# Seven half-width products in place of eight for the gate/up matrix product of a two-layer decoder trunk, and the output product in four chunks

## The chip, the cores and the metric

The kernel runs on one core of a Trainium2 chip. The metric is the time of one execution in device microseconds, the median of several runs; the profile shows one execution in detail. The core has a matrix engine (TensorE, "PE"; its weight loads have a row of their own, "PEld"), VectorE ("DVE"), ScalarE ("ACT"), GpSimd ("POOL"), and SyncE ("SP"), which issues the transfers. Each engine works off its own queue in order; they wait for each other on semaphores.

## The reference

512 tokens of width 1024 go through two layers. A layer is an attention part (one input projection, four heads of differential attention, eight heads of stick-breaking attention, gates, output projections, residual) and then the part that matters here:

```
h2 = rms_norm(x, g_ffn)                                   # 512 x 1024
gate, up = jnp.split(h2 @ w_ffn_in, 2, axis=-1)           # 1024 x 5632 weights
x = x + (jax.nn.silu(gate) * up) @ w_ffn_out              # 2816 x 1024 weights
```

After the second layer comes a last `rms_norm`. All is float32.

## The kernel before

Tokens lie along the free axis: `xs[m]` is a 128x512 tile of `x` (128 channels, 512 tokens), and there are eight of them. Float32 accuracy comes from three matmuls per weight tile: weights and activations are split into a high part (a cast on ACT) and a low part (a subtraction on DVE), and `mm_tiles` (L199 to L206) issues high x high, low x high and high x low into one PSUM bank. `Norm.feed` (L167) makes the split tiles `h` of the scaled `x`; the row factor `r` of the norm comes only from `Norm.finish` (L189) and is multiplied in behind the product.

Weights stream from HBM in pieces of 128x1024 (`w_pieces`, L96): a transfer issued by SP into `wr` (two buffers), the cast to `wh` on ACT (L111), the low part `wl` on DVE (L113; four buffers each). `w_get` (L120) keeps two pieces ahead of the matmuls. `stream` fixes the order of the pieces.

The FFN of a layer (L611 to L642): for each of the 22 hidden tiles `j`, 24 matmuls of 512 columns for gate (`fg`) and 24 for up (`fu`); DVE multiplies both by `r` out of PSUM (L623, L625), ACT takes silu (L624), POOL the product (L626), ACT and DVE split it (L629, L630). Then each of the eight output tiles `fo` sums 22 hidden tiles in one bank (66 matmuls), DVE adds it to `xs[m]` (L639), and the next norm is fed. In the last layer the eighth output tile is done in two halves of 256 tokens (L643 to L665), so that the final norm and the output transfers of the first half run beside the second.

The order in which the instructions stand on each engine's queue is not the order of the code: a scheduler places them when the program is built, by costs of its own, and inserts the waits. Names that recur below: `wh`/`wl` high and low part of a weight piece; `fg`, `fu`, `fo` the PSUM banks of gate, up and output; `yf` the row factor `r`.

## Time and profile before

| | |
|---|---|
| median of 3 runs | 1525.14 us (1522.21 to 1525.25) |
| the profiled execution | 1526.8 us, span of the trace 1525.0 us |
| PE busy | 1488.5 us (98%), 6884 matmuls |
| DVE, ACT, POOL busy | 853.7, 614.4, 347.4 us (56, 40, 23%) |
| granted TensorE clock, mean | 0.988 |

A row of the profile gives engine, line, operation, the tile written and those read, how many, busy time and mean length. Matmuls overlap: a row's length includes the way through the array, so the pace is read from the starts of neighbours. An instruction that waits for a resource inside the engine (not for a semaphore) shows as a longer row.

### The profile page before, as it was taken

The page shows a single profiled execution, that of the slowest core. Times are in us where ns is not written, and L with a number is a line of the kernel's source. Part 1 is how long each engine was busy: PE and PEld are TensorE (multiplying, and loading weights), DVE is VectorE, ACT ScalarE, POOL GpSimd, SP SyncE. Part 2 cuts the span into 40 slices and gives each one's busy share as a digit, 9 for nine tenths or more (in the row PEclk, how much of TensorE's full clock was granted, in tenths as well). Part 3 has the DMA queues.
Part 4 walks back from the last instruction along what each step waited for, and adds up shares of the span by engine and source line. Part 5 has one row for each costly group of instructions (what it writes and reads, how often), then busy time and mean ns, then how long its engine had stood idle before and what let it go on. Part 6 is the DMA issues. An engine that isn't in the chain of part 4 may idle for free.

```text
span 1525.0 us, 17531 instructions
## 1 busy us (share of the span) xinstructions
PE 1488.5 (98%) x6884; PEld 1238.6 (81%) x6884; DVE 853.7 (56%) x1006; ACT 614.4 (40%) x970; POOL 347.4 (23%) x224
## 2 busy tenths in 40 slices
...
DMA packets 43619, 139.59 MB, mean 92 GB/s; under 512 B 5648, under 2 KB 8080, under 8 KB 43536
## 3 DMA queue, kind: packets, MB, share of 16 engines
...
## 4 chain that ended last, share of the span: by engine, by line
PE 90%; DVE 5%; issue 1%; ACT 1%; DMA 1%; POOL 0%; SPq 0%; DVEq 0%; POOLq 0%; ACTq 0%
PE fu L206 5%; PE fg L205 5%; PE fg L206 5%; PE fu L205 5%; PE fg L204 5%; PE fu L204 5%; PE fo L204 5%; PE fo L205 5%; PE fo L206 5%; PE pg L204 4%; PE pg L205 4%; PE pg L206 4%; PE pd L204 3%; PE pd L205 3%; PE pd L206 3%; PE wo L204 2%
## 5 line engine op out<-in xcount | busy, mean ns | idle before, releaser
L111 ACT CAST wh<-wr 128x1024 fp32r<-128x1024 f32 (+3 forms) x251 | 258.0, 1029 | 629.7 <-PE fu L206 157.5
L113 DVE TENSOR_TENSOR wl<-wr,wh 128x1024 fp32r<-128x1024 f32 (+2 forms) x229 | 329.8, 1440 | 216.7 <-ACT wh L111 216.1
L626 POOL TENSOR_TENSOR u<-u,g 128x512 f32<-128x512 f32 x44 | 56.8, 1292 | 441.5 <-DVE u L625 394.3
L205 PE MATMUL fo<-ah,wl 128*128 128x512 f32 (+1 forms) x374 | 141.0, 377 | 0.0
L204 PE MATMUL fo<-ah,wh 128*128 128x512 f32 (+1 forms) x374 | 141.0, 377 | 0.0
L206 PE MATMUL fo<-al,wh 128*128 128x512 f32 (+1 forms) x374 | 140.8, 377 | 0.0
L204 PE MATMUL fg<-hhf,wh 128*128 128x512 f32 x352 | 137.8, 391 | 0.0
L206 PE MATMUL fu<-hlf,wh 128*128 128x512 f32 x352 | 137.0, 389 | 0.0
L205 PE MATMUL fg<-hhf,wl 128*128 128x512 f32 x352 | 137.0, 389 | 0.0
L206 PE MATMUL fg<-hlf,wh 128*128 128x512 f32 x352 | 137.0, 389 | 0.0
L204 PE MATMUL fu<-hhf,wh 128*128 128x512 f32 x352 | 137.0, 389 | 0.0
L205 PE MATMUL fu<-hhf,wl 128*128 128x512 f32 x352 | 137.0, 389 | 0.0
L625 DVE TENSOR_TENSOR u<-fu,yf 128x512 f32<-128x512 f32 x44 | 30.4, 691 | 129.2 <-PE fu L206 129.2
L204 PE MATMUL pg<-hha,wh 128*128 128x512 f32 x256 | 100.5, 392 | 0.0
L205 PE MATMUL pg<-hha,wl 128*128 128x512 f32 x256 | 100.3, 392 | 0.0
L206 PE MATMUL pg<-hla,wh 128*128 128x512 f32 x256 | 100.2, 391 | 0.0
L206 PEld LDWEIGHTS fo<-al,wh 128*128 128x128 f32 x374 | 70.4, 188 | 13.0
L205 PEld LDWEIGHTS fo<-ah,wl 128*128 128x128 f32 x374 | 70.4, 188 | 12.9
L204 PEld LDWEIGHTS fo<-ah,wh 128*128 128x128 f32 x374 | 70.4, 188 | 12.9
L113 POOL TENSOR_TENSOR wl<-wr,wh 128x1024 fp32r<-128x1024 f32 (+3 forms) x22 | 51.9, 2360 | 124.9 <-ACT wh L111 120.4
L204 PE MATMUL pd<-hha,wh 128*128 128x512 f32 x192 | 78.2, 407 | 0.5 <-ACT knd3s L341 0.5
L205 PE MATMUL pd<-hha,wl 128*128 128x512 f32 x192 | 77.7, 405 | 0.0
...
## 6 DMA issues: line engine op xcount, KB each, us to landing
wr<-in_w_fi_dram SPq DMA_DIRECT2D x88, 512.0 KB, 3.6
wr<-in_w_in_dram SPq DMA_DIRECT2D x78, 512.0 KB, 3.7
wr<-in_w_fo_dram SPq DMA_DIRECT2D x32, 512.0 KB, 3.5
wr<-in_w_o_dram SPq DMA_DIRECT2D x16, 512.0 KB, 3.6
wr<-in_w_out_dram SPq DMA_DIRECT2D x16, 512.0 KB, 3.6
...
cs<-in_tab_dram SPq DMA_DIRECT2D x2, 512.0 KB, 5.4
```

What stands on the lines that cost most here:

```text
L111: nc.scalar.copy(out=hi[:, c], in_=raw[:, c])
L113: eng.tensor_tensor(out=lo[:, c], in0=raw[:, c], in1=f32(hi[:, c]), op=ALU.subtract)
L204: nc.tensor.matmul(dst, hi[:, c], rh, start=first and k == 0, stop=False)
L205: nc.tensor.matmul(dst, lo[:, c], rh, start=False, stop=False)
L206: nc.tensor.matmul(dst, hi[:, c], rl, start=False, stop=last and k == n - 1)
L625: nc.vector.tensor_tensor(out=u, in0=bu, in1=r, op=ALU.mult)
L626: nc.gpsimd.tensor_tensor(out=u, in0=u, in1=g, op=ALU.mult)
```

## The change

Only the FFN changes. The hidden tiles 0 and 1 stay as they were ("classic"). The other 20 are computed by the Strassen-Winograd scheme of seven products: the 1024 inputs are divided into even and odd tiles of 128 (four each), the outputs into gate and up, the 512 tokens into two halves. A product (`prod`) is four input tiles x three matmuls of 256 columns, 12 matmuls; seven of them stand in place of 48 matmuls of 512 columns.

For this, four sums of the activations are made once a layer (`sf`, `sh`, `sl`), and for each `j` four sums of the weights (`w_sums`): POOL makes `tf[0]`, `ru[0]`, `tf[1]`, `tf[2]` from the raw pieces `rg` and `ru`, and the split parts are `wh`/`wl` (of `rg`, later of `ru`), `tah`/`tal` (of `tf[0]` and `tf[1]`) and `tbh`/`tbl` (of `tf[2]`). `tf` and `tb` have one buffer. The products of a tile run in the order b11, t1, t2, b21, t3, then, behind the b11 of the next tile, t4 and b22. b11, t2, t3 and t4 go into one bank (`fa`); ACT copies it out after b11, t2 and t3 (`a`, `b`, `c`, 128x256 each), and the next product adds onto the bank. t1 and b22 go into `fc`, b21 into `fb`. DVE and POOL put gate and up together from these. `up` is no longer multiplied by `r`; instead the output product is (`add_x`).

The output product is done in four chunks of 6, 6, 5 and 5 hidden tiles, each behind the first tile of the next chunk. Each chunk's eight tiles are multiplied by `r` on DVE and added into `xs[m]`, on POOL for the first three chunks. Weight pieces of the output product are 768 or 640 columns, 32 a layer in place of 24. In the last layer the last chunk's tiles 4 to 7 are done in two halves of tokens.

```
+CHUNKS = ((0, 6), (6, 12), (12, 17), (17, 22))
+CLASSIC = 2
+EVEN_ODD = (0, 2, 4, 6, 1, 3, 5, 7)
+H = S // 2
...
-    layer_order += [("fi", j) for j in range(2 * NH)]
-    layer_order += [("fo", m, c) for m in range(8) for c in range(3)]
+    FFN = []
+    for c, (j0, j1) in enumerate(CHUNKS):
+        FFN.append(("j", j0))
+        if c:
+            FFN.append(("c", c - 1))
+        FFN += [("j", j) for j in range(j0 + 1, j1)]
+    FFN.append(("c", len(CHUNKS) - 1))
+    for kind, i in FFN:
+        if kind == "c":
+            layer_order += [("fo", m, i) for m in range(8)]
+        elif i < CLASSIC:
+            layer_order += [("fi", 2 * i), ("fi", 2 * i + 1)]
+        else:
+            layer_order.append(("fs", i))
...
+    def w_sums():
+        n = state["next"]
+        state["next"] = n + 1
+        l, _, j = stream[n]
+        fp = state["fp"]
+        pool, tag = (wp, "wr") if j % 2 else (fp, "wx")
+        rg = pool.tile([P, 2, 512], F32, name=f"rg{n}", tag=tag, bufs=2)
+        ru = pool.tile([P, 2, 512], F32, name=f"ru{n}", tag=tag, bufs=2)
+        for t, i in ((rg, 2 * j), (ru, 2 * j + 1)):
+            nc.sync.dma_start(out=t.rearrange("p a k -> p (a k)"), in_=w_fi[l, i])
+        tf = fp.tile([P, 3, 512], F32, name=f"tf{n}", tag="tf", bufs=1)
+        tt = lambda eng, o, a, b: eng.tensor_tensor(out=o, in0=a, in1=b, op=ALU.subtract)
+        def parts(src, pool, tag, bufs, shape):
+            hi = pool.tile(shape, F32R, name=f"{tag}h{n}", tag=tag if pool is wp else tag + "h", bufs=bufs)
+            lo = pool.tile(shape, F32R, name=f"{tag}l{n}", tag="wl" if pool is wp else tag + "l", bufs=bufs)
+            nc.scalar.copy(out=hi, in_=src)
+            nc.vector.tensor_tensor(out=lo, in0=src, in1=f32(hi), op=ALU.subtract)
+            return hi, lo
+        g = parts(rg, wp, "wh", W_BUFS, [P, 2, 512])
+        tt(nc.gpsimd, tf[:, 0], ru[:, 0], rg[:, 0])
+        tt(nc.gpsimd, ru[:, 0], ru[:, 1], ru[:, 0])
+        tt(nc.gpsimd, tf[:, 1], ru[:, 1], tf[:, 0])
+        tt(nc.gpsimd, tf[:, 2], rg[:, 1], tf[:, 1])
+        t = parts(tf[:, 0:2], fp, "ta", 2, [P, 2, 512])
+        u = parts(ru, wp, "wh", W_BUFS, [P, 2, 512])
+        v = parts(tf[:, 2], fp, "tb", 1, [P, 512])
+        at = lambda pr, i: (pr[0][:, i], pr[1][:, i])
+        ready.append((stream[n], dict(b11=at(g, 0), b21=at(g, 1), t1=at(t, 0), t2=at(t, 1), t3=at(u, 0), b22=at(u, 1),
+                                      t4=v), None))
     def w_prefetch():
+        if stream[state["next"]][1] == "fs":
+            return w_sums()
         for _ in w_pieces(1024):
             pass
     def w_get(*key):
-        while len(ready) <= W_AHEAD and state["next"] < len(stream):
+        while state["next"] < len(stream):
+            ahead = sum(2 if r[0][1] == "fs" else 1 for r in ready[1:])
+            if ready and ahead >= W_AHEAD:
+                break
             w_prefetch()
...
+            hq = [h[k] for k in EVEN_ODD]
...
+            for i in range(4):
+                he, ho = F("g", f"he{i}", 2), F("u", f"ho{i}", 2)
+                for t, k in ((he, 2 * i), (ho, 2 * i + 1)):
+                    nc.scalar.activation(out=t, in_=xs[k], func=AF.Copy, scale=pt[:, C_NF + 8 * l + k:C_NF + 8 * l + k + 1])
+                sf = F("wx", f"sf{i}", 2, (P, 4, H))
+                nc.vector.tensor_tensor(out=sf[:, 0], in0=he[:, H:], in1=ho[:, H:], op=ALU.add)
+                nc.gpsimd.tensor_tensor(out=sf[:, 2], in0=he[:, :H], in1=he[:, H:], op=ALU.subtract)
+                nc.vector.tensor_tensor(out=sf[:, 1], in0=sf[:, 0], in1=he[:, :H], op=ALU.subtract)
+                nc.vector.tensor_tensor(out=sf[:, 3], in0=ho[:, :H], in1=sf[:, 1], op=ALU.subtract)
+                sh, sl = F(f"sh{i}", f"sh{i}", 1, (P, 4, H), F32R), F(f"sl{i}", f"sl{i}", 1, (P, 4, H), F32R)
+                nc.scalar.copy(out=sh, in_=sf)
+                nc.vector.tensor_tensor(out=sl, in0=sf, in1=f32(sh), op=ALU.subtract)
+                for q in range(4):
+                    A[f"s{q + 1}"].append((sh[:, q], sl[:, q]))
...
+            def hidden(j, g, u):
                 silu = nc.scalar.activation(out=g, in_=g, func=AF.Silu)
-                nc.vector.tensor_tensor(out=u, in0=bu, in1=r, op=ALU.mult)
-                nc.gpsimd.tensor_tensor(out=u, in0=u, in1=g, op=ALU.mult)
-                hi = fp.tile([P, S], F32R, name=f"ah{j}_{l}", tag="a", bufs=2 * NH)
-                lo = fp.tile([P, S], F32R, name=f"al{j}_{l}", tag="a", bufs=2 * NH)
-                nc.scalar.copy(out=hi, in_=u)
-                nc.vector.tensor_tensor(out=lo, in0=u, in1=f32(hi), op=ALU.subtract)
-                act.append((hi, lo))
+                p = F("p", f"p{j}", 2)
+                (nc.vector if u.space == bass.MemoryType.PSUM else nc.gpsimd).tensor_tensor(
+                    out=p, in0=u, in1=g, op=ALU.mult)
+                hi, lo = F("a", f"ah{j}", 14, dt=F32R), F("a", f"al{j}", 14, dt=F32R)
+                nc.scalar.copy(out=hi, in_=p)
+                nc.vector.tensor_tensor(out=lo, in0=p, in1=f32(hi), op=ALU.subtract)
+                act[j] = (hi, lo)
+                return silu
+            def prod(dst, w, a, first=False):
+                hi, lo = w
+                for k, (ah, al) in enumerate(a):
+                    c = slice(k * P, k * P + P)
+                    for x, y, n in ((hi, ah, 0), (lo, ah, 1), (hi, al, 2)):
+                        nc.tensor.matmul(dst, x[:, c], y, start=first and k + n == 0,
+                                         stop=n == 2 and k == len(a) - 1, skip_group_check=True)
+            class Fast:
+                def __init__(self, j):
+                    self.j = j
+                    self.w = w_get(l, "fs", j)[0]
+                    self.r0 = fbank(f"fa{j}_{l}")[:, :H]
+                    prod(self.r0, self.w["b11"], A["a11"], True)
+                    self.a = self.snap("a")
+                def snap(self, n):
+                    t = F("sn", f"{n}{self.j}", 5, (P, H))
+                    nc.scalar.copy(out=t, in_=self.r0)
+                    return t
+                def middle(self):
+                    j, w = self.j, self.w
+                    self.r2, r1 = fbank(f"fc{j}_{l}")[:, :H], fbank(f"fb{j}_{l}")[:, :H]
+                    prod(self.r2, w["t1"], A["s1"], True)
+                    prod(self.r0, w["t2"], A["s2"])
+                    b = self.snap("b")
+                    prod(r1, w["b21"], A["a12"], True)
+                    self.g, self.u = F("g", f"g{j}", 2), F("u", f"u{j}", 2)
+                    nc.vector.tensor_tensor(out=self.g[:, :H], in0=r1, in1=self.a, op=ALU.add)
+                    nc.gpsimd.tensor_tensor(out=self.g[:, :H], in0=self.g[:, :H], in1=r[:, :H], op=ALU.mult)
+                    prod(self.r0, w["t3"], A["s3"])
+                    c = self.snap("c")
+                    nc.vector.tensor_tensor(out=self.u[:, H:], in0=self.r2, in1=c, op=ALU.add)
+                    self.b = b
+                def tail(self):
+                    w = self.w
+                    prod(self.r0, w["t4"], A["a22"])
+                    nc.vector.tensor_tensor(out=self.g[:, H:], in0=self.r0, in1=r[:, H:], op=ALU.mult)
+                    prod(self.r2, w["b22"], A["s4"])
+                    nc.vector.tensor_tensor(out=self.u[:, :H], in0=self.r2, in1=self.b, op=ALU.add)
+                    return hidden(self.j, self.g, self.u)
+            def add_x(b, m, ts=slice(0, S), eng=None):
+                x = xs[m][:, ts]
+                t = F("p", f"ft{m}", 2)[:, ts]
+                nc.vector.tensor_tensor(out=t, in0=b, in1=r[:, ts], op=ALU.mult)
+                (eng or nc.vector).tensor_tensor(out=x, in0=t, in1=x, op=ALU.add)
+            late = []
+            for kind, i in FFN:
+                if kind == "j" and i < CLASSIC:
+                    bg = fbank(f"fg{i}_{l}")
+                    mm(bg, (l, "fi", 2 * i), hq)
+                    bu = fbank(f"fu{i}_{l}")
+                    mm(bu, (l, "fi", 2 * i + 1), hq)
+                    if i == 0:
+                        r = nrm_f.finish()
+                    g = F("g", f"g{i}", 2)
+                    nc.vector.tensor_tensor(out=g, in0=bg, in1=r, op=ALU.mult)
+                    silu = hidden(i, g, bu)
+                elif kind == "j":
+                    f = Fast(i)
+                    for o in late:
+                        silu = o.tail()
+                    f.middle()
+                    late = [f]
+                elif i < len(CHUNKS) - 1:
+                    for m in range(8):
+                        b = fbank(f"fo{m}{i}_{l}")
+                        mm(b, (l, "fo", m, i), [act[j] for j in range(*CHUNKS[i])])
+                        add_x(b, m, eng=nc.gpsimd)
+            for o in late:
+                silu = o.tail()
...
+            head = [(m, fbank(f"fo{m}{c}_{l}"), w_get(l, "fo", m, c)) for m in range(2)]
+            n = len(aa) - 1
+            for m, b, (hi, lo) in head:
+                mm_tiles(b, hi, lo, aa[:n], True, False)
+            for m in range(4 if last else 8):
+                if m < 2:
+                    _, b, (hi, lo) = head[m]
+                    mm_tiles(b, hi, lo, aa[n:], False, True, n)
+                else:
+                    b = fbank(f"fo{m}{c}_{l}")
+                    mm(b, (l, "fo", m, c), aa)
+                add_x(b, m)
                 nrm.feed(m)
...
+                ws = [w_get(l, "fo", m, c) for m in range(4, 8)]
                 for t in range(2):
                     ts = slice(t * H, t * H + H)
-                    b = fbank(f"fo7{t}")
-                    for c, (hi, lo) in enumerate(w7):
-                        a = [(u[:, ts], v[:, ts]) for u, v in act[8 * c:8 * c + 8]]
-                        mm_tiles(b[:, :H], hi, lo, a, c == 0, c == 2)
-                    x7 = xs[7][:, ts]
-                    nc.vector.tensor_tensor(out=x7, in0=b[:, :H], in1=x7, op=ALU.add)
-                    sq = fp.tile([P, H], F32, name=f"sq7{t}", tag="g", bufs=3)
-                    nc.scalar.activation(out=sq, in_=x7, func=AF.Square)
+                    for m, (hi, lo) in zip(range(4, 8), ws):
+                        b = fbank(f"fo{m}{t}")
+                        mm_tiles(b[:, :H], hi, lo, [(u[:, ts], v[:, ts]) for u, v in aa], True, True)
+                        x = xs[m][:, ts]
+                        add_x(b[:, :H], m, ts)
+                        sq = F("p", f"sq{m}{t}", 2)[:, :H]
+                        nc.scalar.activation(out=sq, in_=x, func=AF.Square)
+                        if m < 7:
+                            acc = nrm.acc[:, ts]
+                            nc.vector.tensor_tensor(out=acc, in0=acc, in1=sq, op=ALU.add)
+                            nc.scalar.activation(out=x, in_=x, func=AF.Copy, scale=pt[:, C_NL + m:C_NL + m + 1])
...
+    w_fi = a["w_ffn_in"].reshape(DEPTH, KT, P, 2 * HID)[:, list(EVEN_ODD)].reshape(DEPTH, D, 2 * HID)
...```

How the change moves instructions is shown at three places. The first is the loop of the fast tiles in layer 0, on ACT, between hidden tiles 7 and 9 (before) and around tile 10 (after; the numbers 75 to 78 on weights are positions in the stream: 76, 77 and 78 belong to tiles 10, 11 and 12). Before:

```order
L624 ACTIVATE g7_0_3998<-g7_0_3998 128x512
L111 CAST wh75_4041<-wr75_4040 128x1024
L629 CAST ah7_0_4004<-u7_0_3999 128x512
L111 CAST wh76_4082<-wr76_4081 128x1024
L624 ACTIVATE g8_0_4070<-g8_0_4070 128x512
```

After:

```order
L150 CAST tbh76_4775<-tf76_4758 128x512
L696 ACTIVATE g9_0_4867<-g9_0_4867 128x512
L150 CAST whh77_4903<-ru77_4887 128x1024
L150 CAST whh78_5023<-rg78_5018 128x1024
L727 COPY b10_0_4985<-fa10_0_4911 128x256
L150 CAST tah77_4899<-tf77_4890 128x1024
L701 CAST ah9_0_4955<-p9_0_4953 128x512
L727 COPY c10_0_5015<-fa10_0_4911 128x256
L727 COPY a11_0_5056<-fa11_0_5043 128x256
L150 CAST tbh77_4907<-tf77_4890 128x512
```

ACT's work for one tile grew from four instructions to nine (the ten rows end with the next tile's `tbh`), and the copies of PSUM (`a`, `b`, `c`) stand behind casts of weight sums.

The second place is the same stretch on POOL, one tile's work (before one row, after six and the next tile's first):

```order
L626 TENSOR_TENSOR u9_0_4143<-u9_0_4143,g9_0_4142 128x512
```

After:

```order
L145 TENSOR_TENSOR tf77_4890<-ru77_4887,rg77_4886 128x512
L145 TENSOR_TENSOR ru77_4887<-ru77_4887 128x512
L145 TENSOR_TENSOR tf77_4890<-ru77_4887,tf77_4890 128x512
L698 TENSOR_TENSOR p9_0_4953<-u9_0_4868,g9_0_4867 128x512
L145 TENSOR_TENSOR tf77_4890<-rg77_4886,tf77_4890 128x512
L739 TENSOR_TENSOR g11_0_5131<-g11_0_5131,yf0_3539 128x256
L145 TENSOR_TENSOR tf78_5022<-ru78_5019,rg78_5018 128x512
```

The first row of the next sum, `tf78`, waits for DVE's `tbl77`, which reads the one buffer of `tf`. On DVE there stand, between `tbl76` and `tbl77` of this stretch, in this order: `u9`, `whl77`, `whl78`, `tal77`, `al9`, `u10`, `g11`, `g10`.

The third place is PE in the same stretch; of each product only the first matmul is shown:

```order
L712 MATMUL fa10_0_4911<-sh0_0_3432,whh76_4771 128x256
...
L712 MATMUL fc11_0_5091<-sh0_0_3432,tah77_4899 128x256
L712 MATMUL fb11_0_5092<-hhf01_3178,whh77_4891 128x256
...
L712 MATMUL fa12_0_5162<-hhf00_3141,whl78_5024 128x256
...
L712 MATMUL fa10_0_4911<-hhf01_3178,tbh76_4775 128x256
...
L712 MATMUL fc10_0_4959<-sh0_0_3432,whh76_4771 128x256
```

These are t3 of tile 10 (it waits for copy `b10`), the first matmul of t1 of tile 11 (waits for `tah77`), b21 of tile 11, b11 of tile 12, t4 of tile 10 (waits for `c10`) and b22 of tile 10. Before, this stretch of PE was one run of `fg` and `fu` matmuls.

## Rows read from the trace of the kernel before

**Rows 1.** Head of the page: span, busy time of each engine, granted clock.

```profile
span 1525.0 us, 17531 instructions
PE 1488.5 (98%) x6884; PEld 1238.6 (81%) x6884; DVE 853.7 (56%) x1006; ACT 614.4 (40%) x970; POOL 347.4 (23%) x224
```

**Rows 2.** Stretches: us, busy and count of PE, PEld, DVE, ACT, POOL; clock; DMA.

```profile
412.00:651.00 239.00, 239.00 (x1054) 197.60 (x1053) 117.78 (x113) 75.28 (x92) 28.42 (x22) 1.00 0.31 96
1513.00:1525.00 12.00, 1.62 (x9) 0.82 (x7) 6.32 (x12) 1.81 (x4) 3.43 (x4) 0.76 0.49 162
```

**Rows 3.** DVE in time, two hidden tiles: start, us, line, operation, idle before.

```profile
424.98 2.12 DVE L113 TENSOR_TENSOR wl<-wr,wh 128x1024 fp32r<-128x1024 f32 x1 [0.40 <-ACT wh L111]
...
429.33 0.69 DVE L623 TENSOR_TENSOR g<-fg,yf 128x512 f32<-128x512 f32 x1 [1.63 <-PE fg L206]
430.42 1.23 DVE L113 TENSOR_TENSOR wl<-wr,wh 128x1024 fp32r<-128x1024 f32 x1 [0.40 <-ACT wh L111]
...
440.21 0.69 DVE L623 TENSOR_TENSOR g<-fg,yf 128x512 f32<-128x512 f32 x1 [1.63 <-PE fg L206]
```

**Rows 4.** PE in time, matmuls of 256 columns, the first and the 65th.

```profile
1496.67 0.28 PE L204 MATMUL fo<-ah,wh 128*128 128x256 f32 x1
...
1504.35 0.28 PE L205 MATMUL fo<-ah,wl 128*128 128x256 f32 x1
```

**Rows 5.** POOL by shape: count, busy us, mean ns, idle before.

```profile
L626 POOL TENSOR_TENSOR u<-u,g 128x512 f32<-128x512 f32 x44 | 56.8, 1292 | 441.5 <-DVE u L625 394.3 <-ACT g L624 47.2
L187 POOL TENSOR_TENSOR accf<-accf,sqf 128x512 f32<-128x512 f32 x10 | 18.5, 1847 | 219.2 <-ACT sqf L185 219.2
L664 POOL TENSOR_TENSOR x<-x,yz 128x256 f32<-128x256 f32 x6 | 5.4, 930 | 30.3 <-DVE yz L156 30.3
```

**Rows 6.** POOL in time, where DVE works beside it.

```profile
10.91 1.32 POOL L113 TENSOR_TENSOR wl<-wr,wh 128x512 fp32r<-128x512 f32 x1 [0.40 <-ACT wh L111]
12.18 1.75 POOL L187 TENSOR_TENSOR acca<-acca,sqa 128x512 f32<-128x512 f32 x1
...
370.93 1.85 POOL L187 TENSOR_TENSOR accf<-accf,sqf 128x512 f32<-128x512 f32 x1 [95.31 <-ACT sqf L185]
...
424.73 1.29 POOL L626 TENSOR_TENSOR u<-u,g 128x512 f32<-128x512 f32 x1 [5.34 <-DVE u L625]
```

**Rows 7.** DVE in time beside these.

```profile
9.75 4.74 DVE L174 SCALAR_TENSOR_TENSOR hla<-x,pt,hha 128x512 fp32r<-128x512 f32 x3 [0.39 <-ACT hha L173]
...
370.88 0.75 DVE L174 SCALAR_TENSOR_TENSOR hlf<-x,pt,hhf 128x512 fp32r<-128x512 f32 x1
```

**Rows 8.** ACT and DVE by shape, the forms that the change uses.

```profile
L111 ACT CAST wh<-wr 128x1024 fp32r<-128x1024 f32 x230 | 242.0, 1053 | 561.2 <-PE fu L206 157.5 <-PE fg L206 113.8 <-PE fo L206 89.5
L629 ACT CAST ah<-u 128x512 fp32r<-128x512 f32 x44 | 27.4, 623 | 45.5 <-POOL u L626 45.5
L428 ACT CAST ths<-ts 128x256 fp32r<-128x256 f32 x16 | 6.1, 379 | 0.6 <-PE ts L425 0.6
...
L630 DVE TENSOR_TENSOR al<-u,ah 128x512 fp32r<-128x512 f32 x44 | 29.8, 678 | 0.0
L398 DVE TENSOR_TENSOR vs<-vts,vs 128x256 fp32r<-128x256 f32 x16 | 6.6, 412 | 1.3 <-ACT vs L397 1.3
```

**Rows 9.** The end: PE's last product, DVE, and ACT's queue of transfers.

```profile
1513.21 0.28 PE L206 MATMUL fo<-al,wh 128*128 128x256 f32 x1
...
1510.96 3.39 DVE L664 TENSOR_TENSOR x<-x,yz 128x256 f32<-128x256 f32 x5
1516.99 0.43 DVE L154 SCALAR_TENSOR_TENSOR tz<-yz 128x256 f32<-128x256 f32 x1 [2.30 <-ACT yz L153]
1518.37 3.35 DVE L664 TENSOR_TENSOR x<-x,yz 128x256 f32<-128x256 f32 x5
...
1511.41 3.31 ACTq L665 DMA_DIRECT2D out_dram<-x  x4
```

**Rows 10.** DMA issues: KB each and us to landing.

```profile
wr<-in_w_fi_dram SPq DMA_DIRECT2D x88, 512.0 KB, 3.6
```

44 lines of the change are left out of this document (17 added, 27 removed).

## The prediction, made before the changed kernel was run

> **What bounds the kernel now.** Three views, in this order. First the busy times: PE is busy for 1488.5 of 1525.0 us, DVE for 56%, POOL for 23% [rows 1]. A busy PE can still be a waiting one, so next the stretch of the FFN: over 239 us of gate and up PE is never idle, at the full granted clock (1.00 of 2.4 GHz), while POOL works 28.4 us of it and DVE 117.8 [rows 2]. Last, the pace: DVE picks up the gate bank of one hidden tile at 429.33 and of the next at 440.21 [rows 3], so a tile's 48 matmuls take 10.88 us, 0.2267 each. The FFN is bound by the number of matmuls, and everything else hides beside it.
>
> **What the seven products take away.** A fast tile has 84 matmuls of 256 columns. The end of the kernel has a run of just such matmuls, float32 in the same pattern of high and low parts, with a fresh weight load for each: the 65th starts 7.68 us after the first [rows 4], 0.120 us each. So 84 x 0.120 = 10.08 us against 10.88: 0.80 us a tile, and for 20 tiles in 2 layers 32 us. This is all that the change can win on PE (half of 0.2267 would be 0.113; the halves cost 0.007 each, or 0.6 us a tile). The output product has the same number of multiplications; its four chunks cost nothing on PE.
>
> The Trainium skill, "TensorE: Matmul & The Clock Gate", section "Back-to-back issue gap", would give 518 and 262 cycles for 512 and 256 columns, 216 and 109 ns; with these figures a tile would win 48 x 0.216 - 84 x 0.109 = 1.2 us and the whole 48 us. The rows of this kernel show 227 and 120, and I go by the rows.
>
> **What has to happen beside a fast tile.** One tile's 10.08 us must now cover, on POOL, four weight sums and the product `p`, all 128x512 from SBUF, at 1.29 each [rows 5], and one 128x256 product by `r`, which the trace shows at 0.93 beside DVE [rows 5]; half of 1.29, 0.65, is my estimate of it alone. That is 7.1 us where it was 1.3. On DVE three low parts of 1024 columns at 1.23 [rows 3], two of 512 at 0.68 and four 256-column additions out of PSUM at 0.41 [rows 8]: 6.7 us. On ACT three casts at 1.05, three of 512 columns at 0.62 (silu taken as the same), three copies of PSUM at 0.38 [rows 8]: 6.2 us. No engine is over 10.08 alone, but POOL and DVE are not independent. The same low part of 1024 columns takes 1.23 us alone and 2.12 when it begins 0.25 us into a POOL product [rows 3, 6]: it ends 1.08 us after POOL does. The other way round a POOL addition takes 1.85 us instead of 1.29 when DVE's `hlf` began 0.05 us earlier [rows 6, 7]. When both have work waiting they alternate: three `hla` take 4.74 us beside two POOL instructions [rows 6, 7]. DVE reading PSUM doesn't disturb: POOL's product at 424.73 has its usual 1.29 [rows 6]. So POOL's 7.1 us and DVE's 3 x 1.23 + 2 x 0.68 = 5.05 us of work on two SBUF operands go nearly one after the other: each handover wins back some 0.13 us (1.85 less 1.29 is 0.56, where `hlf` lasted 0.70 more), which over at most nine handovers leaves 10.9 to 12.1 us a tile, above PE's 10.08.
>
> The Trainium skill, "SBUF — State Buffer", section "Who interferes with whom", says it more strictly: a DVE instruction with two SBUF inputs and a GpSimd instruction that reads SBUF exclude each other for the whole instruction. By that rule a tile can't take less than 12.1 us; by the rows, 10.9.
>
> **The loop that closes.** The queues make it more than a sum. `tf` and `tb` have one buffer, so the sums of one tile start only when `tbl` of the tile before is read, and `tbl` follows the tile's t4. I lay the rows end to end for tile 10, from the end of `tbl76`: POOL `tf77`, `ru77` 2.6; ACT casts `whh77` and `whh78` (they stand ahead of copy `b10`) 2.1, so 4.7; `b10` 0.4: 5.1; PE t3, one matmul, b21, eleven of b11 and t4 are 48 matmuls: 5.8, so 10.9 and 0.16 until the last result is out; ACT `tbh77` 0.6, DVE `tbl77` 0.7: 12.3 us. DVE's other work of that stretch, alternating with POOL (`whl77` from 3.8 to 4.9, then `p9`, `whl78` to 7.2, `tf77`, `tal77` to 9.4, then `al9` and three from PSUM), ends at 11.4, just ahead of `tbl77`. For the period before (tile 9), where `b9` stands ahead of the casts but t1 waits for `tah76` behind them, the same gives 12.1, there by DVE's queue. Value taken: 12.2 us, 2.1 above PE. Bounds: 10.08, if every wait is covered; 11.0, if POOL and DVE did not disturb each other (tile 9's chain without it); 13.4, if the two POOL sums on the chain take 1.85 each instead of 1.29 (1.1 more).
>
> How often is it paid? In each group of fast tiles (2 to 6, 7 to 12, 13 to 17, 18 to 21) PE has a head start: the first sums are made beside classic tiles or an output chunk, and b11 and b21 of the next tile run ahead. The sums of a group's last tile are covered as well, since matmuls of the next output chunk stand between. Counted in PE's order this leaves 3, 3, 2 and 2 periods: 10 a layer, 20 in all, 20 x 2.15 = 43 us of waiting. The transfers don't add to it: a piece may be overwritten once the sums two tiles earlier are done, and it lands 3.6 us after issue [rows 10], some 2 us before its cast.
>
> **The seams.** At the end of layer 0 eight output tiles of 15 matmuls (3.4 us each) replace tiles of 15 us, while DVE now has a multiplication, an addition, the low part of `h` and weight pieces for each, about 2.9 us and POOL's accumulation against it: between 0 and 4 us of waiting for the next layer's first product, taken as 2 since it is nearly full. At the end of the kernel ACT's four transfers of the first half stand ahead of the second half's Exp, and wait for five products of 3.39 us [rows 9]; before, DVE's order let that row run while PE still worked. From the last matmul: `ft7`, an addition, three steps of `yz0`, `x7` and five products end at about 6.1, Exp 6.8, three steps 8.1, five products (3.35) 11.5 us; before, the same five ended 8.5 us after the last matmul (1513.21 to 1521.72) [rows 9]. Three us more; bounds 0 and 5. The activation sums (twelve ACT instructions, DVE's and POOL's) lie beside 21.8 us of classic tiles and cost nothing; without that cover they are some 10 us a layer, which the 13.4 case holds.
>
> **Sum.** -32 + 43 + 2 + 3 = +16, on the profiled execution's own 1526.8 us (1525.0 of span and 1.8 around it): 1543. The median of the runs, 1525.14, lies 1.7 below that execution: 1541 us.
>
> **Rivals.** (1) The waits are mostly covered and it becomes faster. For it: no engine is over 62 to 71% of 10.08 us alone, and PE's order has fillers between t2 and t3. Against: rows 3, 6 and 7. With 11.0 us a period: -32 + 20 x 0.92 + 5 = -9, or 1516; with every wait covered -27, or 1498. It turns to slower once a period is over 11.43 (27/20 above 10.08). Chance 0.27. (2) The two sides cancel: a period near 11.4, 1525 us, within 0.2% (3 us, about what can be told from no change here). Chance 0.10. (3) Slower by more: the waits lengthen to 13.4 us a period, or they bring the granted clock down, as at the end of the kernel, where PE is busy for 1.6 of 12 us and the clock is 0.76 [rows 2]. -32 + 66 + 5 = +39, or 1564. For it: gaps of 1 to 2.5 us every 12. Against: PE would still be busy for four fifths of the time. Chance 0.12. (4) The change doesn't do what it says: half-width matmuls cost as long as their weight loads show, 1238.6/6884 = 0.18 us [rows 1], 15.1 us a tile, +170 us. Against: rows 4 show 0.120 with the same loads. Chance 0.02.
>
> My forecast, slower by 3 to 30 us, has the remaining 0.49. The likeliest case's own range is 1530 to 1555. Faster by over 0.2%: 0.27; within: 0.10; slower: 0.49 + 0.12 + 0.02 = 0.63. The range from 1511 to 1562 leaves out the well-covered part of rival 1 and the far end of rivals 3 and 4, about 2 in 10.
>
> **What would show it.** Right: the 256-column products start 0.120 apart while they run; in the middle of a group from one tile's t4 to the next is about 12.2 us; PE waits before t3 for a copy on ACT, and ACT before that for POOL; POOL's sums show 1.3 to 2.4 us. Wrong: PE without idle time in the groups (then rival 1), POOL's sums at 1.29 beside DVE's low parts, a clock well under 1 in the FFN (rival 3), or an end that takes as long as before.

## The result, and the profile after

The changed kernel takes 1582.79 us (median of 4 runs, 1582.44 to 1584.86), the kernel before 1525.2 beside it: ratio 1.0385, 95% interval 1.0367 to 1.0403. It is slower, as forecast, but by 57.6 us and not by 16; the stated range ended at 1562. The stretches below are read off PE's rows in the two traces, each from its first product to the first product of the next stretch:

| stretch | before, us | after, us | difference |
|---|---|---|---|
| start to the first FFN product of layer 0 | 401.05 | 400.93 | -0.1 |
| FFN of layer 0 | 359.92 | 386.51 | +26.6 |
| attention of layer 1 | 390.74 | 389.16 | -1.6 |
| FFN of layer 1, to the last output product | 361.50 | 387.29 | +25.8 |
| last output product to the end | 11.79 | 16.81 | +5.0 |

Head of the page after, then the stretch of [rows 2] and the kernel's end (us, busy and count of PE, PEld, DVE, ACT, POOL, clock, DMA):

```profile
span 1580.7 us, 21493 instructions
PE 1486.3 (94%) x8318; PEld 1289.2 (82%) x8318; DVE 1073.8 (68%) x1290; ACT 732.5 (46%) x1216; POOL 724.0 (46%) x474
...
412.00:651.00 239.00, 220.38 (x1447) 200.71 (x1447) 160.82 (x164) 96.94 (x145) 147.27 (x98) 0.99 0.28 91
1568.00:1581.00 13.00, 1.22 (x2) 0.50 (x2) 8.32 (x14) 1.40 (x4) 5.38 (x6) 0.50 0.50 162
```

Where PE was never idle it now lacks 18.6 of 239 us; POOL works 147 us there instead of 28. No engine but PE is over 70% busy, and yet PE waits: that has to be looked for in the order of things. First the pace, PE in time, two products with 66 starts from one to the other:

```profile
552.11 0.28 PE L712 MATMUL fb<-hhf,whh 128*128 128x256 f32 x1
...
560.03 0.28 PE L712 MATMUL fa<-hhf,whl 128*128 128x256 f32 x1
```

7.92 us for 66 is 0.120 each, as in [rows 4]. The gain of 16 us a layer is there; 43.3 us of waiting stand against it. To place that waiting, I summed along PE's rows of layer 0 by how much each start comes later than 0.120 us (0.227 for 512 columns) after the one before it. Products that run slowly because the clock is low count in these sums too. "Tile 2 to chunk 0" is the group of fast tiles from tile 2 to the end of output chunk 0, and so on:

| full-width tiles | tile 2 to chunk 0 | tile 7 to chunk 1 | tile 13 to chunk 2 | tiles 18 to 21 | last fast product to layer 1 |
|---|---|---|---|---|---|
| 0.7 | 9.2 | 13.2 | 10.5 | 3.5 | 6.2 |

One period in the middle of a group, from the end of one `tbl` on DVE to the end of the next, POOL in time, then DVE (start, us, operation, idle before and its releaser); the first and the last `tbl` of the DVE rows bound the period before and the one after:

```profile
546.22 1.29 POOL L145 TENSOR_TENSOR tf<-ru,rg 128x512 f32<-128x512 f32 x1 [0.63 <-DVE tbl L151]
547.58 1.28 POOL L145 TENSOR_TENSOR ru<-ru 128x512 f32<-128x512 f32 x1
548.82 1.29 POOL L145 TENSOR_TENSOR tf<-ru,tf 128x512 f32<-128x512 f32 x1
550.07 2.27 POOL L698 TENSOR_TENSOR p<-u,g 128x512 f32<-128x512 f32 x1
552.30 2.27 POOL L145 TENSOR_TENSOR tf<-rg,tf 128x512 f32<-128x512 f32 x1
557.07 0.74 POOL L739 TENSOR_TENSOR g<-g,yf 128x256 f32<-128x256 f32 x1 [2.50 <-DVE g L738]
```

```profile
532.78 1.11 DVE L151 TENSOR_TENSOR tbl<-tf,tbh 128x512 fp32r<-128x512 f32 x1
...
545.01 1.12 DVE L151 TENSOR_TENSOR tbl<-tf,tbh 128x512 fp32r<-128x512 f32 x1
...
549.98 1.23 DVE L151 TENSOR_TENSOR whl<-ru,whh 128x1024 fp32r<-128x1024 f32 x1 [2.48 <-ACT whh L150]
551.12 2.30 DVE L151 TENSOR_TENSOR whl<-rg,whh 128x1024 fp32r<-128x1024 f32 x1
553.34 2.32 DVE L151 TENSOR_TENSOR tal<-tf,tah 128x1024 fp32r<-128x1024 f32 x1
...
557.18 1.18 DVE L151 TENSOR_TENSOR tbl<-tf,tbh 128x512 fp32r<-128x512 f32 x1
...
571.68 0.69 DVE L151 TENSOR_TENSOR tbl<-tf,tbh 128x512 fp32r<-128x512 f32 x1 [0.27 <-ACT tbh L150]
```

From the end of one `tbl` (546.13) to the end of the next (558.36) it is 12.23 us; the value taken in the forecast was 12.2, and 12.1 for this period, which ends with `tbl76`. The period that the prediction laid out in full, `tbl76` to `tbl77`, is the next one: 558.36 to 572.37, 14.0 us against 12.3. The granted clock falls in it (below), which costs about 1.7; the period before (533.89 to 546.13), where ACT has the same order, takes 12.24. Read the starts of the two engines together: 550.07 POOL, 551.12 DVE, 552.30 POOL, 553.34 DVE. Each begins 1.05 to 1.2 us into the other's and ends about as much after it; a pair takes 2.23 us where 1.29 + 1.23 is 2.52. That is the alternation of [rows 6, 7], and DVE reaches `tbl` only behind it. PE in time, three waits of this period and the next, then two rows of ACT:

```profile
548.94 0.39 PE L712 MATMUL fa<-sh,whh 128*128 128x256 f32 x1 [0.46 <-ACT b L727]
551.89 0.39 PE L712 MATMUL fc<-sh,tah 128*128 128x256 f32 x1 [1.25 <-ACT tah L150]
563.17 0.39 PE L712 MATMUL fa<-hhf,whh 128*128 128x256 f32 x1 [2.38 <-ACT whh L150]
```

```profile
548.51 0.37 ACT L727 COPY b<-fa 128x256 f32<-128x256 f32 x1 [2.81 <-PE fa L712]
...
561.12 1.05 ACT L150 CAST whh<-ru 128x1024 fp32r<-128x1024 f32 x1 [3.20 <-POOL ru L145]
```

The names on PE are ACT's. Behind the second and third wait stand casts that wait for POOL's sums. The first wait is another: copy `b` starts as soon as t2 is done (released by PE), and t3 must wait for it, 0.46 us that neither POOL nor DVE causes. After the third and longest of these waits the granted clock falls too. Windows of the same trace, before the wait at 560.6, right behind it, and behind one of 2.34 us that ends at 635.27:

```profile
552.00:560.50 8.50, 8.50 (x71) 8.50 (x72) 6.70 (x8) 2.25 (x5) 5.30 (x5) 1.00 0.37 125
563.20:567.10 3.90, 3.90 (x21) 3.90 (x22) 3.90 (x3) 2.40 (x5) 3.60 (x2) 0.59 0.33 101
635.30:638.80 3.50, 3.50 (x17) 3.50 (x18) 3.50 (x2) 0.76 (x3) 2.50 (x2) 0.55 0.41 151
```

The granted clock is near its lower level of 1.2 GHz (a share of 0.5), and a product takes 0.21 us instead of 0.12: about 1.7 us more for each fall. In the groups it fell three times (also at 1338.8), and not after other waits of 2.3 to 2.7 us (up to 1410.97 and 1421.72). It also fell once in each layer behind the first products of the last chunk (765.3 and 1540.2). A fall doesn't always make the group longer: in layer 1 the group of tile 13 has none and waits 10.6 us, where layer 0's has one and waits 10.5; the waits that follow there are longer by about as much.

How the group of tile 7 begins: POOL in time beside output chunk 0, then one DVE row beside it and DVE's first `tbl`:

```profile
508.98 1.29 POOL L145 TENSOR_TENSOR tf<-ru,rg 128x512 f32<-128x512 f32 x1 [4.38 <-DMA ru<-in_w_fi_dram]
510.23 1.31 POOL L757 TENSOR_TENSOR x<-ft,x 128x512 f32<-128x512 f32 x1
511.49 1.29 POOL L145 TENSOR_TENSOR ru<-ru 128x512 f32<-128x512 f32 x1
...
516.24 2.27 POOL L145 TENSOR_TENSOR tf<-rg,tf 128x512 f32<-128x512 f32 x1
```

```profile
510.69 0.69 DVE L756 TENSOR_TENSOR ft<-fo,yf 128x512 f32<-128x512 f32 x1 [1.84 <-PE fo L261]
...
519.52 1.78 DVE L151 TENSOR_TENSOR tbl<-tf,tbh 128x512 fp32r<-128x512 f32 x1
```

Chunk 0 ends at 514.5, and the first sum begins only at 508.98, released by the transfer of `ru`; in the code these raw halves share buffers with the chunk's weight pieces (raw_first below takes that away). So there is no head start: PE waits from 519 on, in every period of the group. And the last chunk of layer 0, ACT in time, then PE:

```profile
762.12 1.28 ACT L268 ACT_TABLE_LOAD   x1
763.41 0.72 ACT L128 CAST wh<-wr 128x640 fp32r<-128x640 f32 x1
764.27 0.62 ACT L701 CAST ah<-p 128x512 fp32r<-128x512 f32 x1
771.52 1.36 ACT L128 CAST wh<-wr 128x640 fp32r<-128x640 f32 x2 [6.63 <-PE fo L261]
```

```profile
764.19 0.49 PE L259 MATMUL fo<-ah,wh 128*128 128x512 f32 x1 [1.84 <-ACT wh L128]
...
774.16 0.50 PE L260 MATMUL fo<-ah,wl 128*128 128x512 f32 x1 [0.73 <-DVE wl L130]
```

PE ran out of work at 762.2: the fourth piece's cast and the last `ah` stand behind the load of ACT's table, and the next casts behind products that hold all four piece buffers.

### The profile page after: what moved, and what is told of

Its sections match the earlier page's. It is cut to its first block, busy times and chain, and to the rows that moved or that the text cites. A ratio compares the mean times of both kernels' runs of the same rounds, so it can differ in the third digit from the quotient of the medians.

```text
span 1580.7 us, 21493 instructions
## 1 busy us (share of the span) xinstructions
PE 1486.3 (94%) x8318; PEld 1289.2 (82%) x8318; DVE 1073.8 (68%) x1290; ACT 732.5 (46%) x1216; POOL 724.0 (46%) x474
## 5 line engine op out<-in xcount | busy, mean ns | idle before, releaser
L128 ACT CAST wh<-wr 128x1024 fp32r<-128x1024 f32 (+4 forms) x187 | 175.4, 945 | 259.8 <-PE wo L261 44.2
L130 DVE TENSOR_TENSOR wl<-wr,wh 128x1024 fp32r<-128x1024 f32 (+3 forms) x165 | 226.3, 1375 | 58.9 <-ACT wh L128 58.2
L259 PE MATMUL fo<-ah,wh 128*128 128x512 f32 (+1 forms) x372 | 142.5, 387 | 5.6 <-ACT wh L128 4.9
L260 PE MATMUL fo<-ah,wl 128*128 128x512 f32 (+1 forms) x372 | 142.6, 385 | 2.4 <-DVE wl L130 2.4
L261 PE MATMUL fo<-al,wh 128*128 128x512 f32 (+1 forms) x372 | 139.8, 379 | 0.0
L242 POOL TENSOR_TENSOR accf<-accf,sqf 128x512 f32<-128x512 f32 x10 | 18.5, 1847 | 219.3 <-ACT sqf L240 219.3
L757 POOL TENSOR_TENSOR x<-ft,x 128x512 f32<-128x512 f32 x48 | 77.6, 1622 | 83.2 <-DVE ft L756 83.2
L151 DVE TENSOR_TENSOR whl<-ru,whh 128x1024 fp32r<-128x1024 f32 x40 | 56.2, 1405 | 77.4 <-ACT whh L150 77.4
L130 POOL TENSOR_TENSOR wl<-wr,wh 128x1024 fp32r<-128x1024 f32 (+3 forms) x22 | 52.1, 2367 | 105.9 <-ACT wh L128 101.3
L259 PE MATMUL pg<-hha,wh 128*128 128x512 f32 x256 | 100.4, 392 | 0.0
L260 PE MATMUL pg<-hha,wl 128*128 128x512 f32 x256 | 100.3, 392 | 0.0
L261 PE MATMUL pg<-hla,wh 128*128 128x512 f32 x256 | 100.2, 391 | 0.0
L698 POOL TENSOR_TENSOR p<-u,g 128x512 f32<-128x512 f32 x40 | 73.1, 1828 | 39.0 <-DVE u L750 39.0
L259 PEld LDWEIGHTS fo<-ah,wh 128*128 128x128 f32 x372 | 70.6, 190 | 21.3 <-ACT wh L128 8.0
L145 POOL TENSOR_TENSOR tf<-rg,tf 128x512 f32<-128x512 f32 x40 | 87.3, 2183 | 0.8
L145 POOL TENSOR_TENSOR tf<-ru,rg 128x512 f32<-128x512 f32 x40 | 52.8, 1321 | 70.6 <-DVE tbl L151 37.0
L260 PEld LDWEIGHTS fo<-ah,wl 128*128 128x128 f32 x372 | 71.2, 191 | 16.4 <-DVE wl L130 3.9
L151 DVE TENSOR_TENSOR tal<-tf,tah 128x1024 fp32r<-128x1024 f32 x40 | 80.8, 2020 | 4.8 <-ACT tah L150 4.5
L151 DVE TENSOR_TENSOR whl<-rg,whh 128x1024 fp32r<-128x1024 f32 x40 | 78.1, 1953 | 3.6 <-ACT whh L150 3.6
L261 PEld LDWEIGHTS fo<-al,wh 128*128 128x128 f32 x372 | 70.3, 189 | 12.6
L259 PE MATMUL pd<-hha,wh 128*128 128x512 f32 x192 | 77.6, 404 | 0.7 <-ACT knd3s L396 0.7
L150 ACT CAST whh<-ru 128x1024 fp32r<-128x1024 f32 x40 | 42.0, 1051 | 76.5 <-POOL ru L145 71.8
## 6 DMA issues: line engine op xcount, KB each, us to landing
wr<-in_w_in_dram SPq DMA_DIRECT2D x78, 512.0 KB, 3.5
rg<-in_w_fi_dram SPq DMA_DIRECT2D x40, 512.0 KB, 3.5
ru<-in_w_fi_dram SPq DMA_DIRECT2D x40, 512.0 KB, 3.5
wr<-in_w_o_dram SPq DMA_DIRECT2D x16, 512.0 KB, 3.5
wr<-in_w_out_dram SPq DMA_DIRECT2D x16, 512.0 KB, 3.5
wr<-in_w_fi_dram SPq DMA_DIRECT2D x8, 512.0 KB, 3.4
```

What stands on the lines that cost most here:

```text
L128: nc.scalar.copy(out=hi[:, c], in_=raw[:, c])
L130: eng.tensor_tensor(out=lo[:, c], in0=raw[:, c], in1=f32(hi[:, c]), op=ALU.subtract)
L145: tt = lambda eng, o, a, b: eng.tensor_tensor(out=o, in0=a, in1=b, op=ALU.subtract)
L150: nc.scalar.copy(out=hi, in_=src)
L151: nc.vector.tensor_tensor(out=lo, in0=src, in1=f32(hi), op=ALU.subtract)
L242: eng.tensor_tensor(out=self.acc, in0=self.acc, in1=sq, op=ALU.add)
```

## The experiments

Two readings of the 12.2 us stood against each other. "Port" is the name for: POOL and DVE take turns when both work on two SBUF operands, and the room for that is full. "Loop": the single buffers of `tf` and `tb` with the way through ACT and PE close too slowly. Waiting of PE in layer 0's FFN, summed as above (to about 0.2 us):

| run | ratio to before (95%) | tile 2 to chunk 0 | to chunk 1 | to chunk 2 | to last fast | last chunk |
|---|---|---|---|---|---|---|
| the changed kernel | 1.0385 (1.0367-1.0403) | 9.2 | 13.2 | 10.5 | 3.5 | 6.2 |
| two_bufs | 1.048 (1.0464-1.0495) | 13.2 | 12.9 | 12.9 | 6.0 | 6.2 |
| no_low | 1.0065 (1.0049-1.0082) | 5.5 | 4.0 | 2.0 | 2.1 | 6.0 |
| no_sums | 0.9936 (0.9919-0.9953) | 0.1 | 0.1 | 1.7 | 2.2 | 4.6 |
| sums_dve | 1.0132 (1.0114-1.0149) | 7.9 | 5.9 | 5.7 | 1.2 | 5.9 |
| raw_first | 1.033 (1.0313-1.0347) | 9.2 | 8.7 | 7.3 | 7.1 | 6.2 |
| x_dve | 1.0337 (1.0322-1.0352) | 9.1 | 10.4 | 10.6 | 3.4 | 6.0 |
| last_full_pool | 1.0333 (1.0315-1.0352) | 9.2 | 13.2 | 10.6 | 1.9 | 1.7 |
| last_full_dve | 1.014 (1.0122-1.0158) | 6.4 | 6.0 | 6.0 | 1.4 | 1.1 |
| three_of_four | 1.0116 (1.0103-1.013) | 3.4 | 2.9 | 4.8 | 2.7 | 1.0 |
| mixed_pool | 0.9977 (0.9967-0.9987) | 4.7 | 0.5 | 0.3 | 0.1 | 0.0 |
| mixed_dve | 0.9924 (0.9909-0.994) | 2.5 | 0.3 | 0.1 | 0.1 | 0.0 |
| mixed_end | 0.9922 (0.9908-0.9937) | 2.6 | 0.2 | 0.0 | 0.0 | 0.0 |
| two_of_three_dve | 0.9942 (0.9927-0.9956) | 2.4 | 0.2 | 0.0 | 0.0 | 0.0 |
| alternate | 1.0062 (1.0047-1.0077) | 1.5 | 0.0 | 0.0 | 0.0 | 0.0 |
| alternate_dve | 1.0053 (1.0038-1.0068) | 1.2 | 0.0 | 0.0 | 0.0 | 0.0 |
| chunks_only | 1.001 (1.0001-1.0019) | 0.6 | 0.0 | 0.0 | 0.0 | 0.0 |

**two_bufs**, 1599.37 us: two buffers for `tf` and `tb`. To make room it also lowers the kernel's DMA scratch size (`dynamic_dma_scratch_size`) from 1024 to 768; what that does by itself was not tried.

```diff
-        tf = fp.tile([P, 3, 512], F32, name=f"tf{n}", tag="tf", bufs=1)
+        tf = fp.tile([P, 3, 512], F32, name=f"tf{n}", tag="tf", bufs=2)
...
-        v = parts(tf[:, 2], fp, "tb", 1, [P, 512])
+        v = parts(tf[:, 2], fp, "tb", 2, [P, 512])
```

> Two buffers for tf and tb instead of one, nothing else. Theory 'port': the 12.2 us from one tbl to the next in the middle of a group are set by POOL and DVE taking turns (11.3 of the 12.23 us between 546.13 and 558.36 are taken by one or the other working on two SBUF operands); another buffer lets POOL start earlier but adds no room, so a period stays at 11.3 or above and the time falls by at most 0.9 us in some 16 periods a layer: 1555 to 1580 us. Theory 'loop': the single buffers with the legs on ACT and PE set it; with two the period falls to 10.1 to 10.9 us and the time to 1520 to 1540.

The time lies outside both ranges. The loop theory's gain did not come: in the middle of a group the period fell to 11.4 us (`tbl` ends at 542.90 and 554.25), about the 11.3 in which one or the other of the two engines works on two SBUF operands, and not to 10.1 to 10.9. But the kernel became 16 us slower, which neither theory had. POOL now makes the next tile's sums before it has finished the present one's, the first `tbl` of a group comes about 6 us later or more (436.0 against 430.2, 527.5 against 521.3), and t4 waits for ACT (by shape; busy, mean ns, idle before; this run, then the changed kernel):

```profile
L712 PE MATMUL fa<-hhf,tbh 128*128 128x256 f32 x160 | 50.6, 316 | 22.7 <-ACT c L727 22.7
...
L712 PE MATMUL fa<-hhf,tbh 128*128 128x256 f32 x160 | 46.3, 289 | 0.0
```

The order on PE is another one here as well, and the granted clock is lower (0.970 in the mean, 0.983 in the changed kernel), so how much each of these costs stays open.

**no_low**, 1537.52 us: leaves out DVE's three low parts of 1024 columns a tile (nor are their tiles made); the matmuls read the high part in their place.

```diff
-            nc.vector.tensor_tensor(out=lo, in0=src, in1=f32(hi), op=ALU.subtract)
-            return hi, lo
+            if tag == "tb":
+                nc.vector.tensor_tensor(out=lo, in0=src, in1=f32(hi), op=ALU.subtract)
+            return hi, (lo if tag == "tb" else hi)
```

> Leaves out DVE's low parts of rg, ru and tal (three of 1024 columns a fast tile; the high part is used in their place), keeps the four sums on POOL, tbl, all casts, all buffers and all matmuls. Theory 'port': POOL's sums and p show 1.29 us throughout, the period falls to 10.1 to 10.6 us, the time by 50 to 65 us, to 1515 to 1535. Theory 'loop': the way tbl, tf, ru, whh, copy b, t3, t4, tbh, tbl is untouched, the period stays near 12 us and the time at 1565 to 1580.

**no_sums**, 1515.01 us: the four `tt(nc.gpsimd, ...)` lines removed, `t` from `rg`, `v` from `ru[:, 1]`.

> Leaves out POOL's four weight sums (the casts and low parts read the raw halves instead), keeps every instruction of DVE, ACT and PE; the counterpart of no_low. If POOL and DVE taking turns is the cause, DVE's low parts show 1.23 us again, the period falls to 10.1 to 10.5 us and the time to 1515 to 1535, as without the low parts. If no_low was faster only because DVE had less to do, the time stays above 1565.

POOL in time in no_low, a tile's sums and product, nearly all undisturbed:

```profile
537.10 1.30 POOL L145 TENSOR_TENSOR tf<-ru,rg 128x512 f32<-128x512 f32 x1 [1.65 <-DVE tbl L152]
538.48 1.29 POOL L145 TENSOR_TENSOR ru<-ru 128x512 f32<-128x512 f32 x1
539.72 1.29 POOL L145 TENSOR_TENSOR tf<-ru,tf 128x512 f32<-128x512 f32 x1
540.98 1.26 POOL L699 TENSOR_TENSOR p<-u,g 128x512 f32<-128x512 f32 x1
542.21 1.29 POOL L145 TENSOR_TENSOR tf<-rg,tf 128x512 f32<-128x512 f32 x1
```

Without DVE's half of the turns the groups' waiting falls from 36.4 to 13.6 us, with the loop untouched; without POOL's half (and the loop through its sums) to 4.1, with DVE's row untouched. Both times are near the port theory's range of 1515 to 1535 (no_low 2.5 us above it, no_sums at its lower end). So by these two runs about two thirds of the waiting goes with the turns. What no_low keeps, up to 13.6 us a layer, may be the loop's, so the loop theory is not wholly wrong. no_low also takes 3.7 us of work a tile off DVE's queue; that this alone explains its gain is what the next run speaks against.

**sums_dve**, 1546.46 us.

```diff
-        tt(nc.gpsimd, tf[:, 0], ru[:, 0], rg[:, 0])
+        tt(nc.vector, tf[:, 0], ru[:, 0], rg[:, 0])
```

and so the other three sums.

> The four weight sums on DVE instead of POOL. Theory 'port': on DVE the same sum holds the port for 0.68 us instead of 1.29, so a tile needs about 9.5 us of DVE and 2 us of POOL beside it: period 10.8 to 11.5 us, 1530 to 1560 us, and the remaining POOL products p about 1.3 to 2.3 us each. Theory 'loop': the first leg gets 1.2 us shorter, period 11.0: 1540 to 1550. A third view, that DVE's load is what counts (68% of the span already): slower than 1583.

DVE in time, the four sums and two low parts:

```profile
540.87 0.69 DVE L145 TENSOR_TENSOR tf<-ru,rg 128x512 f32<-128x512 f32 x1
541.60 0.69 DVE L145 TENSOR_TENSOR ru<-ru 128x512 f32<-128x512 f32 x1
542.21 0.68 DVE L145 TENSOR_TENSOR tf<-ru,tf 128x512 f32<-128x512 f32 x1
542.93 0.69 DVE L145 TENSOR_TENSOR tf<-rg,tf 128x512 f32<-128x512 f32 x1
543.54 0.42 DVE L750 TENSOR_TENSOR u<-fc,b 128x256 f32<-128x256 f32 x1
543.87 1.22 DVE L151 TENSOR_TENSOR whl<-ru,whh 128x1024 fp32r<-128x1024 f32 x1
545.00 2.32 DVE L151 TENSOR_TENSOR tal<-tf,tah 128x1024 fp32r<-128x1024 f32 x1
```

The busier of the two engines got the work (DVE 73% of the span, POOL 30%), and the kernel is 36 us faster: a sum takes 0.69 us here, and took POOL 1.29 or more. In these rows only `tal`, beside POOL's `p`, is disturbed. A view by load alone is out. Between port and loop this run doesn't decide, since 1546 lies in both ranges.

**chunks_only**, 1527.75 us: `CLASSIC = 22`, and the loop of activation sums removed.

> No fast tile and no activation sums: all 22 hidden tiles by the 48 full-width matmuls, but the output product in four chunks with its additions into x, and the end of the changed kernel. Prices the part of the change that is not Strassen. By the account of the changed trace (end 5 us longer, 6 us of waiting at the last chunk's first products in each layer): 1535 to 1543. If the waiting at the last chunk belongs to the fast tiles that precede it: 1530. If chunks cost nothing: 1525.

The chunked output product is nearly free (+0.1%). The wait at the last chunk is not the chunk's own: here nothing waits there, and ACT's table is loaded at 729.6, beside PE's work. The end is 14.4 us, 2.6 longer than before.

**last_full_pool**, 1575.79 us, and **last_full_dve**, 1546.23 us: tile 21 by full-width products, in the changed kernel and in sums_dve. Both also have the other edits shown further down for the mixed runs (place of the table's load, of the tails, and of the low parts of `w_in`).

```diff
-CLASSIC = 2
+FAST = range(2, 21)
...
```

> The changed kernel itself (sums on POOL, one buffer each) with only the last hidden tile full-width. If the 6 us a layer before the last output chunk belong to the fast last tile: 1582.8 + 1.6 - 11 - what tile 21 waits itself (about 1 a layer) = 1570 to 1574. If they belong to the chunk: 1583.

> sums_dve with one tile less, the last one (21), full-width: 19 fast tiles a layer, sums on DVE. Tells whether the 6 us a layer in front of the last output chunk belong to the last tile's being fast: 1546.5 + 1.6 - 2 x 5.5 = 1537. If they belong to the chunk: 1547. Against mixed_dve it tells whether six more fast tiles are worth having: by sums_dve's 1 us of waiting a fast tile against 0.8 gained, no.

In layer 0 the last chunk's waiting falls from 6.2 to 1.7 and from 5.9 to 1.1, so it belongs to the last tile's being fast; the table's load stands there as in the changed kernel, behind a Silu and ahead of a piece's cast (757.18 in last_full_pool), and PE has products to work on meanwhile. The totals bear it out less well: last_full_pool misses its range (1570 to 1574) by 2 us, and last_full_dve's time is that of the other theory (1547). In layer 1 it gained nothing (FFN 372.8 us against sums_dve's 370.9). In the changed kernel PE's order is the same in both layers; in last_full_dve it differs, and in layer 1 the group of tile 2 waits 9.9 us, with a fall of the clock (0.50 from 1190.6 to 1194.0), for 6.4 without one in layer 0. Whether the order is the cause was not tried.

**raw_first**, 1575.56 us, and **x_dve**, 1576.49 us.

```diff
-        pool, tag = (wp, "wr") if j % 2 else (fp, "wx")
+        pool, tag = (wp, "wr") if j not in (2, 4, 6, 7, 9, 11, 13, 15, 17, 18, 20) else (fp, "wx")
```

```diff
-                        add_x(b, m, eng=nc.gpsimd)
+                        add_x(b, m)
```

> The changed kernel with the raw halves' buffers dealt differently: the first tile after each output chunk (7, 13, 18) reads into the FFN's own pair (wx), not into the pair it shares with the output product's weight pieces (wr); no other edit. In the changed kernel tiles 7 and 13 share with the pieces and their groups wait 13 and 11 us a layer, tile 18 doesn't and its group waits 3. If the late first sums are what took the head start away, the first tbl of these two groups comes 4 us or more earlier and the groups wait about 8 and 6 us: 1582.8 - 20 = 1560 to 1565. If turns of POOL and DVE decide in any case, a period follows on a period and nothing is gained: 1578 to 1585.

> The changed kernel with the output chunks' additions into x on DVE (0.68 each) instead of POOL (1.3 to 2.3), so that they don't stand between the first sums of a group. If POOL's row at the group's beginning is what delays it, 2 to 3 us less in each of 3 groups and 2 layers: 1565 to 1571. If the transfer of ru alone sets the first sum: within 3 us of 1583.

With its own buffers tile 7's `tbl` ends at 498.0 instead of 521.3, and the two groups wait 8.7 and 7.3 us, nearly as the head-start theory has it (8 and 6). But the group of tile 18 waits 7.1 instead of 3.5, so that only 7 of the 20 us are left; why it does is not shown (tile 19 shares with the pieces in both kernels). x_dve wins 2.8 us in one group and nothing in the next. Both times lie between what their two theories gave. In neither run does the clock fall in the group of tile 7, as it does in the changed kernel, so up to 1.7 us of each gain there may be the clock's.

**alternate** (1534.65 us), **alternate_dve** (1533.15 us) and **two_of_three_dve** (1516.21 us) mix fast and full-width tiles; the two with "dve" also have the sums on DVE:

```diff
-CLASSIC = 2
+FAST = range(2, 21, 2)     # two_of_three_dve: [j for j in range(2, 21) if j % 3 != 1]
...
-                if kind == "j" and i < CLASSIC:
+                if kind == "j" and i not in FAST:
                     bg = fbank(f"fg{i}_{l}")
                     mm(bg, (l, "fi", 2 * i), hq)
+                    for o in late:
+                        silu = o.tail()
+                    late = []
                     bu = fbank(f"fu{i}_{l}")
```

> Every second hidden tile fast (2, 4, ... 20: ten a layer), the others with the 48 full-width matmuls, sums on POOL as in the changed kernel, the last tile full-width. If the waits come only from too much POOL and DVE work in 10.08 us, two tiles' 20.96 us of PE cover one tile's 12.2 us of turns and 4 us of the other's, and nothing waits: chunks_only's 1527.75 less 20 x 0.80 = 1512 (1509 to 1516). If a fast tile has waits of its own (the loop from tbl to tbl, the copies), 0.5 to 1 us a fast tile stays: 1522 to 1532.

> As alternate, with the four sums on DVE. With enough time in a pair of tiles it should not matter where the sums run: within 2 us of alternate. If POOL's long sums still delay single steps, up to 5 us faster.

> Two of three hidden tiles fast (13 a layer), the four sums on DVE, the last tile full-width. 31.0 us of PE for three tiles against some 2 x 11 + 4.5 us of turns: covered on the average, so 1527.75 - 26 x 0.80 = 1507 (1505 to 1512); if the second of two neighbouring fast tiles waits as in sums_dve (about 1 us each), 1515 to 1530.

In all three a Silu came behind the load of the norm's table, an error of mine, so that tables were loaded three times at layer 1's start and four times in the end. alternate lies above both of its ranges (1509 to 1516, 1522 to 1532), alternate_dve within 2 us of it, as forecast; two_of_three_dve lies in the range for waits (1515 to 1530), but not by waits, of which it has 2.6 us in layer 0. The alternates' groups hardly wait either: layer 0's FFN, ahead of the tables, took 354 us in both alternates, 6 under before, where 8 were forecast. The rest was lost behind that. Layer 1's attention took 398 and 400 us there for 391, layer 1's FFN gained nothing (362 and 361 us to the last product, 361.5 before), and the end took 5 to 6 us more. With ten fast tiles another set of low parts of `w_in` falls to POOL in layer 1; that is so with thirteen too, where the attention took 389, and it was not tried by itself. **mixed_dve** (1514.03 us) and **mixed_pool** (1520.4 us, two of three tiles fast with the sums on POOL) mend both:

```diff
-            table(LNEXP, silu)
+            with tc.issue_after(tail.ins):
+                table(LNEXP, silu)
...
-            eng = nc.gpsimd if stream[n][1] == "in" and n % 4 == 0 else nc.vector
+            eng = nc.gpsimd if stream[n][1] == "in" and n % len(layer_order) % 4 == 0 else nc.vector
```

> two_of_three_dve with ACT's table for the norms loaded behind both last Silus (there it stood between them, and the tables were loaded four times more at the kernel's end and three times at the start of layer 1, 1.28 us each), and with the low parts of w_in put on POOL in the same rhythm in both layers. FFN as measured there. Two loads a half lie on the end's chain: 1516.2 less 4 (end) less 2 to 4 (seam) = 1508 to 1511. If the loads were hidden: 1515.

> mixed_dve with the four weight sums back on POOL: 13 fast tiles a layer, two of three. If POOL and DVE taking turns sets a fast tile's length, a pair of neighbouring fast tiles waits about 2 us once: 6 pairs in 2 layers, 10 to 20 us over mixed_dve. If a full-width tile in three gives enough room (31.0 us of PE against 2 x 12.2 + 4), it is within 3 us of mixed_dve.

PE's waits by shape (last field), in mixed_dve and then in the changed kernel:

```profile
L712 PE MATMUL fc<-sh,tah 128*128 128x256 f32 x104 | 29.9, 288 | 2.5 <-ACT tah L150 2.5
L712 PE MATMUL fa<-sh,whh 128*128 128x256 f32 x104 | 29.6, 284 | 0.5 <-ACT b L727 0.5
...
L712 PE MATMUL fc<-sh,tah 128*128 128x256 f32 x160 | 47.3, 296 | 15.5 <-ACT tah L150 15.3
L712 PE MATMUL fa<-sh,whh 128*128 128x256 f32 x160 | 48.0, 300 | 13.4 <-ACT b L727 13.4
```

With a full-width tile after every two fast ones the waits are nearly gone, and the time is 0.8% below before (ratio 0.9909 to 0.994). Mending the tables and the low parts won 2 us over two_of_three_dve, so the loads were mostly hidden. The sums' place is worth 6 us here, between the two theories (10 to 20, within 3). **mixed_end** (1513.5 us) is mixed_dve with the first half's output sent from SP alone, and **three_of_four** (1542.78 us) is mixed_end with `j % 4 != 1` in FAST, three fast tiles and then a full-width one:

> mixed_end with three of four hidden tiles fast (15 a layer instead of 13), sums on DVE. If a full-width tile in four still gives DVE and POOL room (41.1 us of PE against 3 x 10.8 + 4.5): 4 x 0.8 = 3 us under mixed_end. If three neighbours wait as in sums_dve, about 1 us a tile: 5 to 15 us over it.

> mixed_dve with all output transfers of the first half issued from SP, so that ACT's row at the kernel's end holds none ahead of the second half's Exp. mixed_dve's end (last output matmul to end) is 14.7 us, 11.8 before the change; if these transfers delay the second half's norm, 2 to 3 us less: 1511 to 1512. If the end waits for the products by the norm on DVE anyway: 1514.

With three fast neighbours the groups wait again, 13.8 us in layer 0, and the time is 29 us over mixed_end, above both ranges. Layer 1's FFN takes 373 us against 363 in layer 0; here too PE's order differs between the layers, and that this is the reason is not shown. The transfers on ACT did not set the end of mixed_dve: mixed_end takes the same time.

## Why the prediction was wrong in size

**What held.** The gain: 0.120 us a product, 16 us a layer. The period: 12.2 us where the clock doesn't fall, and by the way that was laid out, POOL's two sums, ACT's cast, DVE's row behind the alternation. Output chunks nearly free: chunks_only. PE waits before t3 and t1 for ACT and, but for the copy's own way, ACT for POOL; POOL's last sum takes 2.18 us in the mean, the two sums on the chain 1.32 and 1.29. The Trainium skill, "SBUF — State Buffer", section "Who interferes with whom", would have no period under 12.1 us, by an estimate from its rule; two_bufs' 11.4 lies under it and within the 10.9 to 12.1 that the rows gave. One reading was wrong without harm: POOL's product at 424.73 ran beside a low part from SBUF and not beside a read of PSUM. The trace after shows what it was meant to show, at 510.23 (POOL) and 510.69 (DVE out of PSUM), 1.31 and 0.69 us (1.29 and 0.69 alone).

**What failed: "how often is it paid?"** The step took 10 periods a layer, 21.5 us, because each group had a head start and its last tile was covered. The groups waited 36.4 us, as much as 17 periods: 9.2, 13.2, 10.5 and 3.5 where 3, 3, 2 and 2 periods are 6.5, 6.5, 4.3 and 4.3. Only the last group came out. Three parts are seen. The first sums start late, because their raw halves and POOL's row are shared with the output chunk (raw_first takes 7.7 us of waiting from two groups, x_dve 2.8). The last period of a group is not covered: between the last two `tbl` of a group PE still waits 1.9, 1.6, 2.1 and 1.6 us in the four groups, nearly a whole period's 2.15. And the clock fell three times in stretches where I had it at 1.00, about 1.7 us each, in the group of tile 13 without a longer sum. How the 15 us divide among these parts was not measured.

**The seam.** Two us were put at the start of layer 1, where nothing was lost (-1.6). The 6.2 us a layer at the last chunk were in no term; by layer 0 of last_full_pool they belong to the fast last tile, and about 1.7 of them are products at the lower clock.

**The end.** +5.0 for a forecast of +3, at its bound. ACT's transfers, which the forecast blamed, are not it in mixed_end; in the changed kernel itself that was not tried. chunks_only has 2.6, so the halves and the extra multiplications are about half of it, and the rest isn't settled.

With what was measured: -32 + 2 x 36.4 + 2 x 6.2 + 5.0 - 1.6 = 56.6, against 55.7 between the two spans. The rival "slower by more" had the waits at 13.4 us a period, or the clock falling. The period was as forecast and the count wrong; the clock did fall, five times in the two FFNs, which is a small part of the 57.6 us.
